# Retention one block at a time, strewn among the output projection and the last attention, with GpSimd's arithmetic moved elsewhere

## Chip, cores and metric

One core of a Trainium2 chip runs the whole layer. The metric is the device time of one execution in microseconds (us); the median of three runs of the kernel before is 2089.24 us. The engines are PE (matmul), DVE (vector), ACT (scalar), POOL (GpSimd) and SP, whose queue issues most of the plain transfers. Each engine takes its own instructions in the order in which they were written down for it.

## What is computed

One encoder layer over 2048 tokens of width 1024. Cut to what matters here:

```python
xn = rmsnorm(h, attn_norm_g)
q_da, k_da, v_da, q_r, k_r, v_r, g_r = split(xn @ w_in)
o_da = diff_attention(q_da, k_da, v_da, lam, da_subln_g)   # 4 heads, two score maps each, block-causal
o_r = retention(q_r, k_r, v_r, g_r)                        # 4 heads, below
h = h + concat(o_da, o_r) @ w_out
h = h + hier_moe(rmsnorm(h, ffn_norm_g))    # group top-1, expert top-2 of 32 SwiGLU experts
return rmsnorm(h, final_norm_g)

def diff_attention(...):            # per head
    a = p[:, :, 0] - lam * p[:, :, 1]                      # p: the two softmaxed maps
    return rmsnorm(a @ v, subln_g) * 0.8
def retention(q, k, v, g):          # per head, in chunks, decay gamma
    intra = ((q @ k.T) * 0.125 * where(rel >= 0, gamma**rel, 0)) @ v
    cross = (q * gamma**(pos + 1)) @ state
    state = state * chunk_decay + (k * 0.125 * gamma**(last - pos)).T @ v
    return silu(g) * head_rmsnorm(intra + cross)
```

All matrix products of the projections, the values and the experts are made of three matmuls, on a high and a low part of each operand (`mm3`, L62 to L64; `split_psum`, L54 and L55, makes the two parts of something that stands in PSUM).

## The kernel before

The program runs in stages, and a scheduler puts the instructions of each engine in order from a model of the time, with priorities given by the code.

Up to 735 us the input projection (`Proj`, L149 to L260) runs beside most of the attention. It writes q, k, v of the attention and, for retention, RT (q and k transposed), VR and GR to memory. `merge` (L564) mixes two streams of work by weights: the share FA = 0.7 of the attention goes beside the projection, FR = 0.12 beside retention, the rest beside the output projection. Attention runs in three stages over heads; per row block it makes scores (L350, L351, into pS), softmax (L352 to L366 on DVE and ACT), transposes (L382, into pT), values (into pO), and `finish` (L422 to L429) normalises by a Newton iteration and multiplies twice on POOL, by r (L426) and by the gain subg (L427).

Retention (L453) follows from 735 to 864 us. `prepare` loads two blocks of 128 tokens; POOL multiplies v (vd, L481) and q (qd, L486) by their decays; ACT and DVE make the gate th (L490, L491). Per block and pair of heads `inner` multiplies k by q (L499) and transposes k (L500) into one PSUM bank, DVE applies the decay matrix (A, L502) and ACT copies kd (L504); then come the outputs (L523, L524) and the state's increment (L528) in a second bank, which DVE adds to the state (L530). Three banks (pF) serve this. POOL normalises and gates two blocks (L549, L550).

Only then the eight tiles of w_out are loaded (L709) and split (L712 on ACT, L713 on POOL and DVE by turns). From 910 us on, the output projection (`OutProj`) goes block by block beside the last attention stage: `mx` loads a block, `mix` transposes and splits it, `half` multiplies by woh and wol into pF, DVE adds the residual (L747), then norm and router. It waits for attention rows through `k.ready` (L768). From block 12 on it has more PSUM banks (`widen`). The last attention matmul stands at 1168 us, the last block's residual at 1246.

The routing's end goes from 1246 to 1278: the last block's norm (ACT L835, POOL L836), counts and positions on DVE (L977 to L1064), then `route_finish`, which turns the lists by serial rounds of transpose (L1206), copy (L1208), matmul (L1210) and copy (L1211). The gather of the first expert's rows (L1518, POOL's indirect transfer) needs one of these. Weights of the first experts have been loaded ahead; their low parts `ml` are made early by POOL (L1484, L1487) and DVE (L1490).

From 1278 on 32 experts (`Moe`): rows gathered and turned (L1543, L1564), weights split (`mh` L1492 on ACT, `ml` L1493 on DVE), gate and up products, `hidden` (L1598: transposes L1604, then hhi and hlo by `split_psum`), down products, scattering (L1672). A normed and stored column of output runs beside: `f.square` (L1848), scale, store (L1864). In the end `down_last` (L1613) does the last expert and the last two columns, C14 and C15.

## Time and profile before

| | us |
|---|---|
| median of three runs (2086.17 to 2096.96) | 2089.24 |
| the profiled execution | 2073.39 |
| its span, first to last instruction | 2071.5 |
| PE busy | 1940.6 (94%) |
| DVE busy | 1554.3 (75%) |
| ACT busy | 1122.5 (54%) |
| POOL busy | 709.6 (34%) |
| mean granted TensorE clock | 0.975 |

The profiled execution was 15.85 us shorter than the median of the runs. Busy shares are means over the span; a stretch has to be read by itself. Matmuls are pipelined, and their durations overlap: what one costs where nothing waits is the distance between two starts. A releaser in brackets is what ended an engine's idle time.

### The profile page before, as it was taken

How to read it: one execution, taken by the hardware profiler on the slowest of the kernel's cores; microseconds unless marked ns; L12 is line 12 of the kernel's file. 1: busy time of each engine (PE TensorE's matmuls, PEld its weight loads, DVE VectorE, ACT ScalarE, POOL GpSimd, SP SyncE). 2: the span in 40 equal slices, each digit the busy share in tenths (PEclk: the TensorE clock that was granted, in tenths of full speed). 3: DMA queues.
4: the chain of work that ended last, by engine and by line, in shares of the span. 5: the costliest groups of instructions: out<-in, count | busy, mean ns of one | idle time of the engine just before them, and what ended most of it. 6: DMA issues, size and time to landing. Idle time of an engine off the chain costs nothing. (4 is left out here: it accounts for less than half of the span.)

```text
span 2071.5 us, 30117 instructions
## 1 busy us (share of the span) xinstructions
PE 1940.6 (94%) x9811; PEld 1542.1 (74%) x9811; DVE 1554.3 (75%) x3459; ACT 1122.5 (54%) x1915; POOL 709.6 (34%) x369
## 2 busy tenths in 40 slices
PE   7999999999999987789999996999999999999994
PEld 5788888788888875568887774777777677777673
DVE  7345446855566578987877777999998899898985
ACT  4244445544444454555454313776777777776773
POOL 0000000010000037421101106988756578686323
PEclk9999999999999999989999997999999999999997
DMA  6655344573675446464454453999999999999994
GB/s 202 198 150 171 117 133 141 184 236 127 205 214 168 139 154 217 129 198 143 138 171 132 144 227 129 321 321 341 313 322 328 328 321 349 343 356 302 329 309 125
DMA packets 241810, 459.61 MB, mean 222 GB/s; under 512 B 27376, under 2 KB 130160, under 8 KB 240624
## 3 DMA queue, kind: packets, MB, share of 16 engines
q1 hardware_dynamic: 224384, 401.53, 57.4%
q0 software_dynamic: 16976, 55.06, 9.9%
q8 instruction: 78, 1.28, 0.2%
q10 hardware_dynamic: 288, 1.05, 0.1%
q14 instruction: 84, 0.69, 0.1%
HBM read 365.81 MB, written 91.75 MB: 221 GB/s over the span
## 5 line engine op out<-in xcount | busy, mean ns | idle before, releaser
L1493 DVE TENSOR_TENSOR ml<-mr,mh 128x1024 fp32r<-128x1024 f32 x376 | 446.1, 1211 | 34.4 <-ACT mh L1492 34.2
L1492 ACT ACTIVATE mh<-mr 128x1024 fp32r<-128x1024 f32 x376 | 383.9, 1054 | 115.7 <-PE acc L74 70.5
L1525 POOL DMA_INDIRECT xg<-XN,TA x120 | 281.4, 2345 | 55.6 <-issue 30.8
L352 DVE CUSTOM_DVE_ANT_0 p<-pS,dist 128x512 f32<-128x512 f32 (+1 forms) x320 | 188.0, 605 | 124.8 <-PE pS L351 118.3
L426 POOL TENSOR_TENSOR U<-U,r 128x512 f32<-128x512 f32 (+2 forms) x13 | 16.5, 1271 | 724.8 <-DVE r L40 622.8
L359 ACT ACTIVATE p<-p,nm 128x128 f32<-128x128 f32 (+15 forms) x128 | 153.8, 1202 | 112.6 <-DVE nm L358 112.4
L62 PE MATMUL acc<-mh,xhi 128*128 128x512 f32 x512 | 204.7, 402 | 0.6 <-ACT xhi L1566 0.6
L63 PE MATMUL acc<-ml,xhi 128*128 128x512 f32 x512 | 204.1, 399 | 0.2 <-DVE ml L1493 0.2
L64 PE MATMUL acc<-mh,xlo 128*128 128x512 f32 x512 | 202.7, 397 | 0.7 <-DVE xlo L1567 0.7
L54 ACT ACTIVATE ah<-pT 128x512 fp32r<-128x512 f32 (+2 forms) x176 | 85.4, 498 | 139.2 <-PE pT L382 99.8
L62 PE MATMUL pa<-whi,xh 128*128 128x512 f32 x384 | 152.2, 398 | 3.0 <-ACT whi L161 2.3
L62 PE MATMUL pa<-xh,whi 128*128 128x512 f32 x384 | 152.7, 398 | 2.0 <-DVE st L58 2.0
L63 PE MATMUL pa<-wlo,xh 128*128 128x512 f32 x384 | 153.2, 400 | 1.5 <-DVE wlo L162 1.5
L64 PE MATMUL pa<-whi,xl 128*128 128x512 f32 x384 | 153.8, 401 | 0.0
L63 PE MATMUL pa<-xl,whi 128*128 128x512 f32 x384 | 152.0, 396 | 0.0
L64 PE MATMUL pa<-xh,wlo 128*128 128x512 f32 x384 | 151.7, 395 | 0.0
L350 PE MATMUL pS<-kst,qs 128*128 128x512 f32 (+1 forms) x320 | 124.7, 402 | 18.8 <-DVE cm L352 7.8
L162 DVE TENSOR_TENSOR wlo<-wr,whi 128x1024 fp32r<-128x1024 f32 x72 | 90.7, 1261 | 66.2 <-ACT whi L161 66.0
L55 DVE TENSOR_TENSOR al<-pT,ah 128x512 fp32r<-128x512 f32 (+2 forms) x176 | 97.5, 564 | 44.1 <-ACT ah L54 43.7
L62 PEld LDWEIGHTS acc<-mh,xhi 128*128 128x128 f32 x512 | 96.3, 188 | 31.8 <-ACT xhi L1566 0.7
L161 ACT ACTIVATE whi<-wr 128x1024 fp32r<-128x1024 f32 x72 | 76.1, 1058 | 80.1 <-DMA wr<-in_w_in_dram 39.9
L351 PE MATMUL pS<-kst,qs 128*128 128x512 f32 (+1 forms) x320 | 115.4, 376 | 0.0
(540 smaller groups left out, 4915.1 us busy)
## 6 DMA issues: line engine op xcount, KB each, us to landing
mr<-in_expert_w_gate_dram SPq DMA_DIRECT2D x128, 512.0 KB, 5.8
mr<-in_expert_w_up_dram SPq DMA_DIRECT2D x128, 512.0 KB, 6.2
mr<-in_expert_w_down_dram SPq DMA_DIRECT2D x128, 512.0 KB, 7.4
wr<-in_w_in_dram SPq DMA_DIRECT2D x72, 512.0 KB, 4.7
vst<-VS SPq DMA_DIRECT2D x72, 256.0 KB, 5.1
qs<-QS SPq DMA_DIRECT2D x128, 128.0 KB, 4.0
st<-in_x_dram SPq DMA_DIRECT2D x16, 512.0 KB, 4.2
VS<-st SPq DMA_DIRECT2D x32, 256.0 KB, 3.0
```

Of the source, the lines that this page charges most:

```text
L55: return nc.vector.tensor_sub(lo, ps, hi.bitcast(F32))
L62: nc.tensor.matmul(out, s_hi, m_hi, start=start, stop=False)
L63: nc.tensor.matmul(out, s_hi, m_lo, start=False, stop=False)
L64: nc.tensor.matmul(out, s_lo, m_hi, start=False, stop=stop)
L162: nc.vector.tensor_sub(lo, r, hi.bitcast(F32))
L350: nc.tensor.matmul(x, qs[0][:, m, 0, o:o + 128], ks[m][:, a0:a1], start=True, stop=False)
L351: nc.tensor.matmul(x, qs[0][:, m, 1, o:o + 128], ks[m][:, a0:a1], start=False, stop=True)
L352: nc.vector.tensor_tensor_reduce(p[:, a0:a1], x, tab[:, c0 + a0:c0 + a1], SLOPES[h], -3.0e38, OP.add, OP.max, accum_out=cm[:, n:n + 1])
L359: nc.scalar.activation(p[:, :nk], p[:, :nk], AF.Exp, bias=nm, accum_out=s0 if m == 0 else s1)
L1492: self.hi_at = nc.scalar.activation(hi, r, AF.Copy)
L1493: self.lo_at = nc.vector.tensor_sub(lo, r, hi.bitcast(F32))
L1525: nc.gpsimd.indirect_dma_start(out=xg[:, g * 256:(g + 1) * 256], out_offset=None, in_=v, in_offset=bass.IndirectOffsetOnAxis(ap=ix[:, g], ...
```

## The change

Retention is written for one block at a time, in `beside` with the last 0.3 of the attention, and both run beside the output projection. Keys are divided by their decay when the projection stores them (`key_decay`), so that q and v need no decay, the score needs only a mask, and the state's increment only a factor for each head (on ACT, while it copies kd). The norm's epsilon is scaled per row instead (`edec`). The gate is made when GR is stored, and applied by DVE, head by head. Retention has one PSUM bank (pR), the output projection two instead of three until `widen`; the last attention stage has smaller pools. w_out is loaded as soon as the projection ends; the gain subg goes into its first four tiles.

```diff
@@ Proj, storing RT and GR
+                nc.vector.tensor_mul(st..., ps..., k.kdec[:, ct - 2, None, :].to_broadcast([128, 4, 128]))
...
+                nc.scalar.activation(st, ps, AF.Tanh, scale=0.5)
+                nc.vector.scalar_tensor_tensor(st, st, 1.0, ps, op0=OP.add, op1=OP.mult)
@@ finish
-        nc.gpsimd.tensor_mul(u, u, r[:, :, None].to_broadcast([128, n, 128]))
-        nc.gpsimd.tensor_mul(u, u, k.subg[:, None, :].to_broadcast([128, n, 128]))
+        nc.vector.tensor_mul(u, u, r[:, :, None].to_broadcast([128, n, 128]))
-    step = 2 if (s, h) == (len(STAGES) - 1, 3) else nq
+    step = 2 if end else nq
@@ retention
-        G.tensor_mul(X.vd, ...)
...
-            G.tensor_mul(qd, ...)
...
+        pa = k.pR.tile([128, 512], F32, name="pR")
+        V.tensor_mul(A, pa[:, :256]..., k.msk[:, None, :].to_broadcast([128, 2, 128]))
+            nc.scalar.activation(kd[:, s], pa[:, 256 + 64 * s:320 + 64 * s], AF.Copy, scale=math.exp(128 * LGAM[2 * pr + s]))
...
-            G.tensor_mul(O, O, r[:, :, :, None].to_broadcast([128, 2, 4, 128]))
-            G.tensor_mul(O, O, X.th.rearrange("p a (h e) -> p a h e", h=4))
+        for h in range(4):
+            V.scalar_tensor_tensor(th[:, h], O[:, h], r[:, h:h + 1], th[:, h], op0=OP.mult, op1=OP.mult)
+        k.kept = b + 1
@@ OutProj
-BP = ((3, 2), (3, 1), (3, 2))
+BP = ((3, 2), (3, 1), (2, 1))
-        k.pF = pool("pF2", 3, space=PSUM)
+        k.pF = banks("pF2", 2)
+        k.pR = banks("pR", 1)
-        (nc.gpsimd if t % 2 < WOP else nc.vector).tensor_sub(lo, r, hi.bitcast(F32))
+            nc.scalar.activation(hi, r, AF.Copy, scale=k.subg)
+            nc.vector.scalar_tensor_tensor(lo, r, k.subg, hi.bitcast(F32), op0=OP.mult, op1=OP.subtract)
-            while b >= k.ready or b == LAST - 1 and not k.att_done:
+            while b >= min(k.ready, k.kept) or b == LAST - 1 and not (k.att_done and k.kept == NB):
-            nc.gpsimd.tensor_mul(xn, xn, k.ffg)
+            nc.vector.tensor_mul(hg, ht, k.ffg)
+            nc.scalar.activation(self.xn, hg, AF.Copy, scale=r)
@@ the stages
-        merge(tc, retention(k), 58, a, na * FR)
-        merge(tc, op.blocks(at), OB, a, na * (1 - FA - FR))
+        b = beside(retention(k), nr, a, ns)
+        merge(tc, op.blocks(at), OB, b, nr + ns)
```

In the routing's end, `route_finish` puts four transposes into one bank, copies them once and makes ten matmuls from the copy. All early weight splits are DVE's: three behind that copy, the rest behind the first rows' split.

```diff
@@ Moe
-            if 2 * q + part < EG:
-                nc.gpsimd.tensor_sub(lo, r, hi.bitcast(F32))
...
+            with k.tc.issue_after((k.turned if 2 * q + part < EL else k.split0).ins):
+                nc.vector.tensor_sub(lo, r, hi.bitcast(F32))
-        self.hl_at = split_psum(nc, X.hh, X.hl, pt)
+        self.hh_at = nc.scalar.activation(X.hh, pt, AF.Copy)
+        self.hl_at = nc.vector.tensor_sub(X.hl, pt, X.hh.bitcast(F32))
@@ the experts
+        with tc.high_priority(FIRST):
+            m.gather(jobs[0])
+            m.rows(jobs[0])
...
+                    with tc.high_priority(HID):
+                        m.hidden(jobs[n - 1])
...
-        with tc.issue_after(m.silu.ins):
+        m.hidden(X)
+        with tc.issue_after(m.hh_at.ins):
             f.square(C[13])
-        m.hidden(X)
+FIRST = 400
+HID = 200
```

The scheduler decides what this does to the order. First PE, before: a piece of the retention stretch. pS are attention scores, pT its transposes; the rest is retention.

```order
L382 MATMUL pT<-ident,p_7157 128x128 x2
L350 MATMUL pS<-kst,qs 128x512
L351 MATMUL pS<-kst,qs 128x512
L499 MATMUL pF<-qz_8149,kt 128x256
L500 MATMUL pF<-ident,kt 128x128
L523 MATMUL pF<-state_8155,qd_9150 128x128
L524 MATMUL pF<-vr,A 128x128
```

PE after, in the output projection beside the last attention. pF with woh and wol is the output projection, its L875 row the transposes for the router, pO the attention's values; L359 and L360 are its scores under their new line numbers.

```order
L62 MATMUL pF<-woh,mh 128x512
L63 MATMUL pO<-al,vst 128x128
L64 MATMUL pO<-ah,vst 128x128
L63 MATMUL pF<-wol,mh 128x512
L64 MATMUL pF<-woh,ml 128x512
L875 MATMUL pF<-ident,ht 128x128 x4
L527 MATMUL pR<-state_8190,qz_8194 128x128
L528 MATMUL pR<-vr,A 128x128
L530 MATMUL pR<-vr,kd 64x128
L359 MATMUL pS<-kst,qs 128x512
L360 MATMUL pS<-kst,qs 128x512
```

Retention's matmuls (pR) now stand in small groups between rows of the output projection and of attention. Next PE in the routing's end, ahead of the first expert, before: pF are the lists of `route_finish`, L1543 turns the first expert's rows.

```order
L1217 MATMUL pF<-P,LG 128x32 [waits Activation_49]
L1217 MATMUL pF<-P,LG 128x32 x3
L1206 MATMUL pF<-ident,aia 32x128
L1210 MATMUL pF<-P,atia_13367 128x32 [waits DVE_49]
L1206 MATMUL pF<-ident,aib 32x64 [waits PE_49]
L1210 MATMUL pF<-P,atib_13375 64x32 [waits DVE_49]
L1217 MATMUL pF<-P,LG 128x32 [waits Activation_49]
L1217 MATMUL pF<-P,LG 128x32
L1206 MATMUL pF<-ident,aib 32x64
L1210 MATMUL pF<-P,atib_13388 64x32 [waits DVE_49]
L1543 MATMUL pt<-ident,xg 128x128 [waits DMASW0_49,DVE_49]
```

And after, with L1226, L1238 and L1241 for the lists and L1561 for the rows:

```order
L1226 MATMUL pF<-ident,aia 32x128 [waits DVE_49,PE_49]
L1226 MATMUL pF<-ident,aia 32x128 [waits DVE_49]
L1226 MATMUL pF<-ident,aib 32x64 [waits DVE_49] x2
L1238 MATMUL pF<-P,at 128x32 [waits DVE_49]
L1238 MATMUL pF<-P,at 128x32
L1238 MATMUL pF<-P,at 64x32 x2
L1241 MATMUL pF<-P,LG 128x32 [waits Activation_49]
L1241 MATMUL pF<-P,LG 128x32 x3
L1241 MATMUL pF<-P,a_13574 128x32 [waits Activation_49]
L1241 MATMUL pF<-P,a_13574 128x32
L1561 MATMUL pt<-ident,xg 128x128 [waits DMASW0_49]
```

The serial rounds, each with a wait for DVE, have become one group; the turning of the rows waits for the gather alone. Last, ACT near the end, before: sg is the last expert's gate, fo the square of column C13, hhi the last hidden rows.

```order
L1658 ACTIVATE y<-acc 128x512 [waits PE_49]
L1585 ACTIVATE sg<-acc 128x512 [waits PE_49]
L1848 ACTIVATE fo,fs<-fh 128x1024 [waits DMASW6_49]
L54 ACTIVATE hhi<-pt 128x512 [waits DVE_49,PE_49]
L1630 ACTIVATE fo,fs_20994<-fh 128x512 [waits DMASW0_49,DVE_49,Activation_49]
L1630 ACTIVATE fo,fs_20994<-fh 128x512 [waits DVE_49]
L1633 ACTIVATE fo,fs_20995<-fh 128x1024 [waits DMASW1_49,Activation_49]
```

After:

```order
L1512 ACTIVATE mh<-mr 128x1024 [waits DMAHW2_49,DVE_49]
L1603 ACTIVATE sg<-acc 128x512 [waits PE_49]
L1623 ACTIVATE hhi<-pt 128x512 [waits PE_49]
L1872 ACTIVATE fo,fs<-fh 128x1024 [waits DMASW6_49]
L1650 ACTIVATE fo,fs_21198<-fh 128x512 [waits DMASW0_49,DVE_49,Activation_49]
L1652 ACTIVATE fo,fs_21199<-fh 128x1024 [waits DMASW1_49,Activation_49]
L1650 ACTIVATE fo,fs_21198<-fh 128x512 [waits DVE_49,Activation_49]
```

hhi (L1623) has moved ahead of the square of C13 (L1872).

## Rows read from the trace of the kernel before

**Rows 1.** Page: engine, busy us, share of the span, instructions.

```profile
PE 1940.6 (94%) x9811; PEld 1542.1 (74%) x9811; DVE 1554.3 (75%) x3459; ACT 1122.5 (54%) x1915; POOL 709.6 (34%) x369
```

**Rows 2.** Windows: length, busy PE, PEld, DVE, ACT, POOL, clock, DMA, GB/s.

```profile
735.00:864.00 129.00, 105.27 (x688) 83.93 (x687) 107.15 (x299) 69.10 (x252) 71.82 (x42) 0.95 0.55 175
864.00:910.00 46.00, 27.46 (x132) 22.37 (x130) 41.84 (x85) 23.76 (x48) 20.30 (x8) 0.74 0.54 183
...
735.00:905.00 170.00, 127.98 (x798) 102.57 (x797) 143.99 (x374) 88.75 (x289) 88.77 (x50) 0.90 0.56 179
...
910.00:1168.00 258.00, 251.14 (x1601) 211.93 (x1602) 194.46 (x559) 123.01 (x225) 37.44 (x30) 1.00 0.46 147
...
1246.00:1278.00 32.00, 13.64 (x65) 10.16 (x65) 24.10 (x101) 12.22 (x17) 17.62 (x9) 0.56 0.28 99
...
1290.00:1450.00 160.00, 154.82 (x688) 117.38 (x687) 159.50 (x214) 116.31 (x137) 142.01 (x53) 1.00 0.96 329
```

**Rows 3.** Timeline of PE, output projection: start us, us, engine, line, operation, tiles.

```profile
960.06 0.40 PE L62 MATMUL pF<-woh,mh 128*128 128x512 f32 x1
960.30 0.39 PE L63 MATMUL pF<-wol,mh 128*128 128x512 f32 x1
```

**Rows 4.** Timeline of PE, retention; a row with x2 holds two matmuls.

```profile
754.09 0.39 PE L523 MATMUL pF<-state,qd 128*128 128x128 f32 x2
754.31 0.39 PE L524 MATMUL pF<-vr,A 128*128 128x128 f32 x2
```

**Rows 5.** Waits, 735 to 910: who for whom, us in total, times, longest.

```profile
ACT junk L533 <- DVE state L530: 25.4, 14, 6.8
```

**Rows 6.** Timeline of SP's queue: start, time to issue, transfers.

```profile
879.25 20.62 SPq L709 DMA_DIRECT2D wor<-in_w_out_dram  x8
```

**Rows 7.** Groups on DVE by form, 735 to 905: busy us, mean ns, idle before.

```profile
L491 DVE SCALAR_TENSOR_TENSOR th<-th,gr 128x1024 f32<-128x1024 f32 x8 | 11.3, 1407 | 2.2 <-ACT th L490 2.2
L530 DVE SCALAR_TENSOR_TENSOR state<-state,sdec,pF 128x128 f32<-128x128 f32 x30 | 10.2, 339 | 6.0 <-PE pF L528 5.7
```

**Rows 8.** Line L363, 735:905, then 910:1168: ns minimum/median/maximum, first and last start.

```profile
L363 DVE SCALAR_TENSOR_TENSOR c<-c,S,nlam x6: 212/1124/1944, 751.6 to 891.1; 128x1 f32<-128x1 f32 x6
...
L363 DVE SCALAR_TENSOR_TENSOR c<-c,S,nlam x11: 204/221/1336, 914.6 to 1137.2; 128x1 f32<-128x1 f32 x11
```

**Rows 9.** POOL's costliest group, 735 to 905.

```profile
L550 POOL TENSOR_TENSOR O<-O,th 128x1024 f32<-128x1024 f32 x8 | 22.3, 2790 | 0.3
```

**Rows 10.** Timeline of DVE, routing end.

```profile
1250.95 2.23 DVE L990 TENSOR_TENSOR pen<-m,c 128x8 f32<-128x8 f32 x1
...
1260.38 2.33 DVE L1232 TENSOR_SCALAR aia<-RUN,ppia 128x32 f32<-128x32 f32 x1
...
1262.83 0.22 DVE L1232 TENSOR_SCALAR aib<-RUN,ppib 64x32 f32<-64x32 f32 x1
```

**Rows 11.** Timeline of POOL, routing end.

```profile
1250.81 2.34 POOL L836 TENSOR_TENSOR xn<-xn,ffg 128x1024 f32<-128x1024 f32 x1 [68.62 <-ACT xn L835]
1255.64 7.02 POOL L1484 TENSOR_TENSOR ml<-mr,mh 128x1024 fp32r<-128x1024 f32 x3 [2.49 <-ACT mh L1482]
1269.54 1.11 POOL L1518 DMA_INDIRECT xg<-XN,fia  x1 [6.88 <-PE pF L1206]
```

**Rows 12.** Timeline of PE, routing end; transfers, 1265 to 1280, us to landing.

```profile
1276.32 1.97 PE L1543 MATMUL pt<-ident,xg 128*128 128x128 f32 x8 [0.28 <-DVE wb L1211]
...
xg<-XN,fia POOLq DMA_INDIRECT x1, 4.5
```

**Rows 13.** Waits of PE, 1310 to 2037.

```profile
PE acc L64 <- DVE hlo L55: 6.9, 6, 2.6
```

**Rows 14.** Timeline, end of the program.

```profile
2041.48 1.06 ACT L1848 ACTIVATE fo<-fh 128x1024 bf16<-128x1024 f32 x1 [6.37 <-DMA fh<-H,perm]
...
2043.16 0.79 PE L62 MATMUL acc<-mh,hhi 128*128 128x512 f32 x1 [5.71 <-ACT hhi L54]
...
2044.19 1.00 POOL L1839 DMA_INDIRECT fh<-H,perm  x1 [5.24 <-DMA H<-y,ia]
```

More of the change, by code (lines that the diff above doesn't have):

```diff
@@ L445, in att_head @@
                 done += step
-                if step == 2:
+                if end and h == 3:
                     k.ready = 4 * g0 + done
@@ new lines, in load, with inner @@
+        return X
+    def inner(X, pr):
+        kT = X.kt[:, pr]
+        pa = k.pR.tile([128, 512], F32, name="pR")
+        nc.tensor.matmul(pa[:, :256], kT, X.q[:, pr], start=True, stop=True)
+        nc.tensor.transpose(pa[:, 256:384], kT, k.ident)
+        A = k.br.tile([128, 2, 128], F32, name="A")
+        V.tensor_mul(A, pa[:, :256].rearrange("p (s c) -> p s c", s=2), k.msk[:, None, :].to_broadcast([128, 2, 128]))
+        kd = k.br.tile([128, 2, 64], F32, name="kd")
+        for s in range(2):
+            nc.scalar.activation(kd[:, s], pa[:, 256 + 64 * s:320 + 64 * s], AF.Copy, scale=math.exp(128 * LGAM[2 * pr + s]))
+        return A, kd
@@ L517, in retention @@
+    nxt = load(0)
+    yield R0
+    for b in range(NB):
+        X = nxt
+        th = k.br.tile([128, 4, 128], F32, name="th", bufs=1)
+        nc.sync.dma_start(th, k.GR[X.ts, :].rearrange("p (h e) -> p h e", h=4))
+        O = k.br.tile([128, 4, 128], F32, name="O", bufs=1)
+        ss = k.br.tile([128, 4], F32, name="ss4")
+        st = []
+        for pr in range(2):
+            st.append(inner(X, pr))
+            yield 0.6
+        if b + 1 < NB:
+            nxt = load(b + 1)
         for pr in range(2):
@@ L902, in mixers @@
     with ExitStack() as ctx:
-        k.br = ctx.enter_context(tc.tile_pool(name="br", bufs=2, side="right", reuse_waits="tile"))
-        k.pF = ctx.enter_context(tc.tile_pool(name="pF", bufs=3, side="right", reuse_waits="tile", space=PSUM))
-        ret_consts(k)
-        merge(tc, retention(k), 58, a, na * FR)
-    with ExitStack() as ctx:
+        k.kept = 0
         op = OutProj(k, ctx, outer)
@@ new lines, in route_finish @@
+    p4 = ps()
+    o = 0
+    for i, (tab, p0, n, idx, w) in enumerate(lists):
+        for c in range(2):
+            x = 64 * i + 32 * c
+            nc.tensor.matmul(p4[:n, x:x + 32], at[:, o:o + n], k.P, start=True, stop=True)
+            o += n
+    for g in range(6):
+        nc.tensor.matmul(p4[:, 128 + 32 * g:160 + 32 * g], a4[g // 4][:, g % 4 * 128:g % 4 * 128 + 128], k.P, start=True, stop=True)
+    for i, (tab, p0, n, idx, w) in enumerate(lists):
+        q = (k.TA if idx == "ia" else k.TBw).bitcast(I32)[:, 0:n // 32]
+        setattr(k, idx + "q", q)
+        V.tensor_scalar(q, p4[:, 128 + 128 * i:128 + 128 * i + n].rearrange("p (g e) -> p g e", e=32), 4.0, k.quad,
+                        op0=OP.mult, op1=OP.add)
```

325 lines of the change are left out of this document (144 added, 181 removed).

## The prediction, made before the changed kernel had run

> **What bounds the kernel now.** I read the busy shares first: PE is busy 94% of the span and DVE 75% [rows 1], so a gain must come out of a stretch in which PE stands still or works thinly. The windows by stage name two such stretches [rows 2]. From 735 to 905 us (retention with some attention, then the wait for w_out) PE is busy 128 of 170 us at a mean granted clock of 0.90, with POOL busy 88.8 us; from 1246 to 1278 (the end of the routing) PE is busy 13.6 of 32 us, at 0.56. From 910 to 1168 (output projection with the last attention) it is busy 251 of 258 at 1.00.
>
> Busy time flatters PE, since ends are modelled. I therefore count its dense content: so many matmuls from the instruction order, times their spacing where nothing waits. That spacing is 0.23 us for 512 columns [rows 3] and 0.11 us for a retention matmul of 128 columns (pairs 0.22 apart) [rows 4]. 735 to 864 then holds 92 us of PE work in 129, 864 to 910 holds 15 in 46, 910 to 1168 about 243 in 258: 350 us of work in 433, or 81%. What PE lacks up to 864 is shown by who waits: ACT stood 25.4 us for DVE's state update, 14 times, the longest 6.8 [rows 5]. From 864 to 910 PE lacks w_out: SP spends 20.6 us issuing its eight loads, from 879.25 on [rows 6].
>
> **Retention in the output projection.** PE's retention work stays: 64 matmuls of 256 columns at 0.22, 280 of 128 at 0.11, 60 for the state at about 0.16, in all 54 us. It was packed between 735 and 864; by the new order it is strewn between attention scores and w_out matmuls. Counted in the new order, PE has 19.5 us of dense work between the projection and the first w_out matmul, 301 from there to the last retention matmul and 32 to the last attention matmul: 352, as before. Each piece is priced by its own limit.
> - Head: 19.5 us of PE, but about 39 of DVE (eight splits of w_out and the attention beside them), and 20.6 of SP for w_out before that. I take 45 us; the bounds are 39 (DVE alone) and 60 (w_out's 20.6 first, DVE's 39 behind it).
> - Mixed part: 301 us at an efficiency that no row shows. Neighbours are 71% (735 to 864) and 94% (910 to 1168). I take 91%, near the second, because the queued w_out matmuls are there to fill, as they were after 910, but one retention bank and two instead of three for w_out are less freedom: 331 us.
> - Tail: 32 of PE against 46 of DVE: 48.
>
> The sum is 424 against 433, -9. Behind the last attention the order has 61 us of PE work up to the experts where it had 67: -6. Region: **-15**, from -42 (head 39, 97%) to +27 (head 60, 84%).
>
> This needs DVE to have room, for all that GpSimd did now falls on it, ACT or nobody. Before, DVE was busy 107+42+194 = 343 us from 735 to 1168 [rows 2]. Added: 64 gating operations at 0.34 (the nearest row is the 128x128 state update) are 22, four more w_out splits at 1.4 (the 128x1024 row) are 6, more normalisations of the last attention 8. Moved into the projection: eight operations of 1.41 us [rows 7], -11; there they become 24 shorter ones, in a stretch where DVE has room and PE doesn't wait for it, so I cost them at 0 (bounds -3 and +3; without that cover, 14). Given back: DVE is slower next to POOL. A one-column operation (L363) takes 0.22 us at the median in the output projection and 1.12 in retention, with a longest of 1.94 [rows 8]; POOL's own run up to 2.8 us [rows 9]. The excess of every DVE form over the same form elsewhere, added up in this way, is 33 us, of which these six make 5. DVE ends at about 335 us in 424: 79%, as busy as before (343 in 433), so I keep it off the path except in head and tail.
>
> The Trainium skill (SBUF — State Buffer, "SBUF: two separate sides") says that DVE and GpSimd share a port pair as an exclusive lock, so that the loser stands for the whole instruction. The L363 row agrees in kind. By that rule alone up to the whole POOL time of the stretch, 88.8 us, could come back to DVE instead of 33, and nothing of DVE's would be late; the sum keeps 33.
>
> Retention's loads go from two blocks to one (SP has some 70 issues more). SP is not what ends PE's waits there, so 0, bounds -1 and +4: behind w_out's loads in SP's queue now stand the first block's loads, inside the head's 45.
>
> **Routing tail.** DVE's small operations stretch beside POOL: 2.23 us for an 8-column one, and three others up to the 32-column 2.33, whose twin takes 0.22 [rows 10]. Beside them POOL runs the last normed block and three weight splits [rows 11]. The four cost 8.9 us and alone 0.7: -8.2, on the chain to the gather's index. The gather is issued at 1269.54, but PE turned the rows only at 1276.32, because four serial rounds of transpose, copy and matmul stood before it (released by the last copy, not by the gather) [rows 12]. Batched, those rounds end first, and the gather's landing (4.5 us after issue) decides: 1269.5-8.2+4.5 = 1265.8, 10.5 earlier. Then 1.5 goes back: three more splits at 1.4 us fall on DVE behind the first split of rows, where DVE is busy 159.5 of 160 us [rows 2], and PE only partly hides it. **-9**, from -12 to -4.
>
> **Experts and end.** The transposes of the hidden rows come earlier; PE waited 6.9 us in six places for the lower half of the split [rows 13]: **-5**, bounds -9 and +4 (earlier transposes can push a weight split behind on a full DVE). At the end ACT stood for a load until 2041.48 with the hidden rows' split queued behind it, and PE until 2043.16, 5.7 us idle [rows 14]. The new order puts that split first. But the next block's load is issued at 2044.19, when the scatter of the rows before has landed, and the last adds wait for it as they do for PE: I count 2 of the 5.7. **-2**, from -4 to 0. The remaining small moves lie on no chain that the trace shows: 0.
>
> **The sum.** -15-9-5-2 = -31 us, 2073.39 to about 2042 for the profiled execution. That one lies 15.85 us (0.8%) below the median of the runs, 2089.24; I take the same difference off the median: **2058 us**. Something like 0.5%, 10 us, is what a measurement here can tell from no change.
>
> **Rivals.**
> *A, the mixed part runs dense.* If the freed DVE and the strewn retention let PE run at 97% with a head of 39 us, the region is 39+310+46 = 395, less 6: -44 and in all -60, 2029. If both happen in part, -45. For: 910 to 1168 had 94% with DVE at 75%, and of POOL's 88.8 us more than 33 may come back to DVE. Against: one retention bank, two w_out banks. 0.20.
>
> *B, retention is only moved.* Head and tail, both at DVE's pace, take back what the stretch of 735 to 905 gives: region 0 (head 58, 90% in between, tail as forecast, -6 behind), half of the routing's gain lost on a DVE that is full from 1290 on, the earlier transposes nothing, the end -2: -6, 2083. For: DVE has 39 and 46 us in head and tail, and K, V and w_out loads fall together. Against: the routing's rows are plain. 0.18.
>
> *C, slower: the one retention bank.* PE takes its instructions in order. A block passes the bank four times, 64 times in all, and PE stands until DVE and ACT have emptied it. In the new order most passes are 1.5 to 10 us of other PE work apart, about a dozen less than 1. Emptying takes at least the 0.34 of DVE and ACT's copies behind it; a DVE that is 80% full adds what is queued ahead, and one long row operation is over 2 us. At 0.5 us a pass the forecast holds (its 30 us of loss). From about 1 us a pass (61 lost, the forecast's 30 and its gain of 31) the kernel is slower than before; at 1.3, 83 are lost and it ends at 2111. For: the retention stretch itself worked so, at 71%, with three banks. Against: the spacing. 0.09.
>
> There PE would also stop shortly and often. In 735 to 905 its mean granted clock was 0.90, against 1.00 afterwards [rows 2]. The Trainium skill (TensorE: Matmul & The Clock Gate, "A second HAM failure mode: psum-queue depth-cycling") tells of a kernel in which cycling through PSUM banks left PE such short idles that the clock kept falling; by that rule, an estimate, a mixed part at 0.90 would cost up to a tenth of its 301 us more. The trace shows the lower clock beside longer waits too, so I leave it inside C.
>
> **How the numbers follow.** Forecast 0.53 (2045 to 2074: the region from -28 to 0, the rest as summed), A 0.20, B 0.18, C 0.09. Faster by over 0.5% takes the forecast and A but for a small part of the forecast's upper edge, and a little of B: 0.75. Same: 0.16. Slower: C, 0.09. For 8 in 10 the range reaches through A's middle and B: 2020 to 2090, leaving out the far end of A and C.
>
> **What would show it.** First w_out matmul near 780; last attention matmul near 1160; PE busy shares above 9 tenths between them at a clock of 1.00, with waits for pR of a few us in all. L363 back at 0.22 everywhere. DVE from the last residual add to the expert's first transposes without a 2 us row, the transposes some 10 us closer, released by the gather. No wait of 5 us ahead of the last down matmuls. Waits on pR or A of tens of us would show C; a head over 55 us shows B. The prediction is wrong if the projection up to 735 or the weight-bound experts move by more than 5 us, for which I see no reason.

## The result and the profile after

The changed kernel took 2139.96 us (median of four runs, 2126.19 to 2147.03) against 2088.77 us before: a ratio of 1.0247, interval 1.0209 to 1.0284. It is slower by 51 us, and the forecast was 31 us faster. The profiled execution took 2136.21 us, its span 2134.4, where before had 2071.5. The spans differ by 63 us and not by 51 because the profiled execution of before lay some 15 us below its median, that of after 4 us below.

To see where the 63 us between the two spans lie, I cut both traces at the same events of PE (its first or last matmul of a kind):

| stretch | before, us | after, us | difference |
|---|---|---|---|
| start to last projection matmul | 734.7 | 762.8 | +28.1 |
| to first w_out matmul (head) | 175.8 | 48.8 | |
| to last retention matmul (mixed) | | 353.4 | |
| to last attention matmul (tail) | 255.0 | 62.0 | |
| from the projection's end to the last attention matmul | 430.8 | 464.3 | +33.5 |
| to last w_out matmul | 79.6 | 83.3 | +3.7 |
| to first expert matmul | 33.0 | 26.1 | -6.9 |
| to last expert matmul | 772.9 | 771.1 | -1.8 |
| to the end | 20.5 | 26.8 | +6.3 |

One trace stands behind each column. How firm the rows are is shown by traces with the same order on PE: two versions of before that are edited only from the routing on (below) end the projection at 736.4 and 735.7 and take 431.2 and 435.1 us to the last attention matmul, so the left column holds within 5 us there. The changed kernel and five edits of it that leave PE's order in the projection as it is end it between 754.0 and 763.5, so its +28.1 may be 19 to 29.

The windows of after, by stage, with the columns of [rows 2]:

```profile
0.00:763.00 763.00, 728.62 (x3621) 608.96 (x3622) 452.02 (x1260) 333.85 (x666) 7.10 (x48) 0.98 0.54 164
763.00:812.00 49.00, 35.01 (x159) 25.81 (x157) 33.01 (x98) 21.68 (x58) 0.00 (x0) 0.69 0.84 259
812.00:1165.00 353.00, 330.26 (x2021) 269.59 (x2020) 254.50 (x888) 162.58 (x420) 26.02 (x20) 0.98 0.47 148
1165.00:1227.00 62.00, 45.43 (x267) 35.84 (x265) 41.91 (x119) 26.45 (x50) 4.59 (x4) 0.81 0.14 49
1227.00:1310.00 83.00, 72.58 (x364) 55.61 (x365) 55.82 (x302) 14.19 (x33) 0.00 (x0) 0.90 0.53 194
1310.00:1337.00 27.00, 14.11 (x70) 10.62 (x69) 19.80 (x107) 12.49 (x18) 8.38 (x5) 0.61 0.28 93
```

POOL is out of the way, as it was to be, and DVE has what was forecast (33+254.5+41.9 = 329 us, 335 forecast). The head is 49 us long (45 forecast). But the mixed stretch is 353 instead of 331, the tail 62 instead of 48 at a granted clock of 0.81, and the projection, for which nothing was forecast, is 28 us longer. DVE's stretching beside POOL, on which part of the gain was to rest, is indeed gone: the one-column operation of [rows 8] and the 8-column one of [rows 10] read, in after (minimum/median/maximum ns),

```profile
L372 DVE SCALAR_TENSOR_TENSOR c<-c,S,nlam x16: 211/216/221, 816.1 to 1198.8; 128x1 f32<-128x1 f32 x16
...
L1009 DVE TENSOR_TENSOR pen<-m,c x1: 156/156/156, 1316.3 to 1316.3; 128x8 f32<-128x8 f32 x1
```

So that mechanism works, and the kernel lost elsewhere. Splitting PE's time tells how. For each form of matmul I took its usual distance to the next start (the 30th percentile in that trace, or the distance itself where shorter) as its work, the time in which PE was empty as idle, and the remainder as rest (half clock, waits inside the pipeline):

| from the projection's end to the last attention matmul | length | work | idle | rest |
|---|---|---|---|---|
| before | 430.8 | 307.5 | 49.2 | 74.1 |
| after | 464.3 | 328.2 | 53.3 | 82.7 |

Two things are seen: idle and rest, 123 us before, are 136 now, not less; and nearly the same matmuls (2441 records where before had 2404) have become 21 us more work. The idle time has changed its kind: 31.5 us of it ended at an operation of DVE before and 18.0 after, 8.9 us at a load before and 22.0 after. The experiments take these one by one, then the projection and the routing. Stretches are quoted by their cuts: "projection" is the time of its last matmul, "mixed stretch" is from there to the last attention matmul (464.3 in the changed kernel).

### The profile page after: what moved, and what is told of

Same layout as the page of the kernel before. It is cut to its first block, busy times and chain, and to the rows that moved or that the text cites. A ratio compares the mean times of both kernels' runs of the same rounds, so it can differ in the third digit from the quotient of the medians.

```text
span 2134.4 us, 30383 instructions
## 1 busy us (share of the span) xinstructions
PE 1982.5 (93%) x9811; PEld 1564.9 (73%) x9811; DVE 1563.1 (73%) x3684; ACT 1118.5 (52%) x1927; POOL 575.9 (27%) x293
## 4 chain that ended last, share of the span: by engine, by line
PE 76%; DMA 9%; DVE 5%; issue 4%; POOL 2%; ACT 2%; SPq 1%; DVEq 0%; ACTq 0%; POOLq 0%
PE pa L62 7%; PE pa L63 7%; PE pa L64 7%; PE acc L63 7%; PE acc L64 7%; PE acc L62 7%; PE acc L72 4%; PE acc L74 3%; PE pS L359 3%; PE pF L62 3%; PE pF L63 3%; PE pF L64 3%; PE pS L360 3%; PE pT L391 2%; PE pO L63 1%
## 5 line engine op out<-in xcount | busy, mean ns | idle before, releaser
L1543 POOL DMA_INDIRECT xg<-XN,TA x120 | 272.2, 2268 | 54.0 <-issue 30.5
L359 PE MATMUL pS<-kst,qs 128*128 128x512 f32 (+1 forms) x320 | 124.4, 404 | 27.8 <-DMA qs<-QS 14.6
L887 POOL TENSOR_TENSOR xc<-xT 128x512 bf16<-128x512 f32 x24 | 30.6, 1277 | 432.4 <-ACT xT L884 429.4
```

What stands on the lines that cost most here:

```text
L359: nc.tensor.matmul(x, qs[0][:, m, 0, o:o + 128], ks[m][:, a0:a1], start=True, stop=False)
L1543: nc.gpsimd.indirect_dma_start(out=xg[:, g * 256:(g + 1) * 256], out_offset=None, in_=v, in_offset=bass.IndirectOffsetOnAxis(ap=ix[:, g], ...
```

## Experiments on the mixed stretch

**The state's matmuls.** In the new text each head's increment (L530, 64 rows of output) stands behind that head's output; before, both heads' increments stood together (L528). The edit puts them together again:

```diff
-                if b < NB - 1:
-                    nc.tensor.matmul(po[s * 64:(s + 1) * 64, 256:384], kd[:, s], v, start=True, stop=True)
             if b < NB - 1:
+                for s in range(2):
+                    h = 2 * pr + s
+                    nc.tensor.matmul(po[s * 64:(s + 1) * 64, 256:384], kd[:, s], X.vr[:, h * 128:(h + 1) * 128], start=True, stop=True)
```

> The two matmuls that make the state's increment of a pair of heads (64 output rows each, in two halves of the bank) stand next to each other again behind the outputs, as before the change, instead of one behind each head's output. Theory P (adjacent they run at the same time on two halves of the array; apart each takes its own 0.16 us and more): these 120 matmuls, 30.9 us from start to next start in the changed kernel, fall to 18 to 22, the stretch from the projection's end to the last attention matmul from 464 to 450 to 458, total -6 to -13. Rival: the waits around them take the time instead, and the stretch stays within 4 us.

The mixed stretch fell to 449.8 (-14.5), its work to 310.3; the total to 2121.9 us (ratio to before 1.0147, 1.0103 to 1.0191). Timelines of PE, first the changed kernel, one pair of heads, then this one:

```profile
871.64 0.38 PE L527 MATMUL pR<-state,qz 128*128 128x128 f32 x2
871.86 0.39 PE L528 MATMUL pR<-vr,A 128*128 128x128 f32 x2
872.18 0.43 PE L530 MATMUL pR<-vr,kd 128*64 128x128 f32 x2
872.54 0.49 PE L527 MATMUL pR<-state,qz 128*128 128x128 f32 x2
872.86 0.39 PE L528 MATMUL pR<-vr,A 128*128 128x128 f32 x2
873.18 0.43 PE L530 MATMUL pR<-vr,kd 128*64 128x128 f32 x2
```

```profile
864.48 0.38 PE L527 MATMUL pR<-state,qz 128*128 128x128 f32 x2
864.70 0.39 PE L528 MATMUL pR<-vr,A 128*128 128x128 f32 x2
864.92 0.39 PE L527 MATMUL pR<-state,qz 128*128 128x128 f32 x2
865.14 0.39 PE L528 MATMUL pR<-vr,A 128*128 128x128 f32 x2
865.46 0.44 PE L532 MATMUL pR<-vr,kd 128*64 128x128 f32 x4
```

A pair takes 1.9 us in the first (871.64 to the end of 0.36 us behind 873.18), 1.4 in the second. One such matmul shows as two records, so 120 records are 60 matmuls, and a row with x2, in [rows 4] too, is one matmul. The increments of both heads, four records, end in 0.44 us when adjacent, and their starts lie 0.01 us apart by twos; alone, the two records of one take 0.36 to the next start. Over all 120 records the distances to the next start sum to 17.6 us before, 30.9 after and 21.7 here. Theory P holds, and it is most of the 21 us of added work (17.9 go with this edit).

**The order of output projection and attention.** OB is the weight of the output projection in `merge`; a smaller one lets attention and retention go ahead.

```diff
-OB = 200
+OB = 150
```

> The weight OB of the output projection in the merge is 150 instead of 200, so attention and retention run earlier beside it. Theory T: the stretch from the last retention matmul to the last attention matmul (62 us) shrinks below 50 and the whole by 10 to 20 us. Theory S: the order of loads is as crowded, total within 6 us of the changed kernel. Theory B: within 6 us.

Total 2123.14 us (1.0185, 1.0122 to 1.0247), mixed stretch 445.2 (-19), idle in it 40.6 instead of 53.3; the part that ended at a load is 9.4 us instead of 22.0. The tail did not shrink (75 us, since retention ends earlier), so theory T is right about the knob and wrong about the place. What the wait rows of PE show (us in total, times, longest) is fewer waits for loads of qs and kst (those for mx stay: 5.6 us); after, then this run:

```profile
PE pS L359 <- DMA qs<-QS: 11.8, 5, 4.4
PE pT L391 <- DVE p L375: 7.6, 2, 6.0
PE pS L359 <- DMA kst<-KS: 5.2, 1, 5.2
PE pF L765 <- DMA mx<-MIX: 5.1, 3, 2.4
...
PE pR L528 <- ACT O L536: 3.1, 1, 3.1
```

```profile
PE pS L359 <- DMA qs<-QS: 4.2, 2, 4.0
PE pS L359 <- DMA kst<-KS: 3.9, 1, 3.9
```

**The one retention bank** (rival C of the prediction).

```diff
-            po = k.pR.tile([128, 512], F32, name="pR")
+            po = k.pR.tile([128, 512], F32, name="pF")
...
-        k.pF = banks("pF2", 2)
-        k.pR = banks("pR", 1)
+        k.pF = k.pR = banks("pF2", 3)
```

> Retention and output projection share three PSUM banks (pF) instead of one and two. Theory B (one retention bank makes PE wait): total 10 to 30 us less than the changed kernel, in the stretch from the projection's end to the last attention matmul. Theories S and T: within 6 us, since PE's waits for pR sum to some 10 us in the changed kernel.

2137.06 us (1.0279, 1.0218 to 1.034), mixed stretch 459.2. Within the 6 us that the other theories gave; rival C falls. PE's waits had said so: in the changed kernel those for pR sum to 9.7 of 53 us, and the longest is the 3.1 above.

**SP's queue.** Between 860 and 1140 us SP stood 57 us (20 times) for buffers of retention's q loads, with loads of attention queued behind. The loads kt, qz, vr and th go to POOL's queue:

```diff
-            nc.sync.dma_start(X.kt[:, pr], k.RT[2 + pr][:, ts])
+            nc.gpsimd.dma_start(X.kt[:, pr], k.RT[2 + pr][:, ts])
...
```

> Retention's loads (kt, qz, vr, th) are issued by POOL instead of SP; nothing else is edited. Theory S (SP's queue: retention's loads wait there for free buffers, and the loads of attention and output projection stand behind them; PE waits for those loads and runs at half clock after): from the end of the projection to the last attention matmul 464 us become 430 to 445, PE's waits for qs, kst and mx fall from some 20 us to under 8, total 20 to 30 us less than the changed kernel. Theory T (the last attention runs alone at the end, since the output projection has used up its blocks): 464 stays within 6 us. Theory B (one retention bank): stays within 6 us.

2141.24 us (1.0275, 1.0224 to 1.0326), mixed stretch 469.1. Theory S, my first after the result, falls. The same with the stores that wait for DVE (GR and both halves of MIX):

```diff
-            nc.sync.dma_start((k.VR if c == 4 else k.GR)[bs, :], st)
+            (nc.sync if c == 4 else nc.gpsimd).dma_start((k.VR if c == 4 else k.GR)[bs, :], st)
...
-        nc.sync.dma_start(k.MIX[X.ts, 512:1024], th.rearrange("p h e -> p (h e)"))
+        nc.gpsimd.dma_start(k.MIX[X.ts, 512:1024], th.rearrange("p h e -> p (h e)"))
```

> The changed kernel with the stores that wait for DVE (the gate GR in the projection, both halves of MIX) issued by POOL instead of SP. Theory Q (these stores hold SP's queue while they wait for DVE, weight and key loads stand behind them, and PE waits): the projection ends at 745 to 752 instead of 754 to 763, the stretch to the last attention matmul falls by 8 to 20 from 464, total 2115 to 2130. Rival: as with retention's loads, nothing changes by more than 6 us, since other waits take the place.

2138.43 us (1.0233, 1.0202 to 1.0264), projection 761.1, mixed stretch 464.0: the rival. Taking these waits out of SP's queue gives PE nothing.

**Together.** Pairs, lambda's tile (below), OB = 150, and the early splits behind the first rows (below):

> The changed kernel with four of the edits tried together: the state's matmuls in pairs, lambda's own tile in the first two stages, OB = 150, early splits behind the first rows. If the gains add up (-14 in the stretch by the pairs, -5 at the start by lambda, -19 by OB, -2 by the splits): total about 2095 to 2105, from the projection's end to the last attention matmul 425 to 435, level with the kernel before or up to 1% slower. If they are one gain seen several times (the last attention's order): total 2110 to 2120.

2110.99 us (1.012, 1.0088 to 1.0152): projection 751.3, mixed stretch 432.9, experts 790.0. The mixed stretch is now level with before (430.8); the expected 2095 to 2105 was missed by what the experts lost. A good part of that came with the fourth edit: PE's first 96 expert matmuls took 48.5 us instead of 38.1, with a hole of 12.65 us that is explained with the early splits below. The version without that edit was not run. On this one three more; first a smaller OB:

```diff
-OB = 150
+OB = 100
```

> The version with four edits with OB = 100 instead of 150. Theory T (attention ends late because the output projection has used up its blocks): the stretch from the projection's end to the last attention matmul falls from 433 to 410 to 425, total -8 to -20 against 2111. Rival: at OB = 150 this is spent; total within 6 us of 2111 or longer, because then output projection work is left for later with nothing beside it.

2115.93 us (1.0145, 1.0117 to 1.0173), mixed stretch 433.8: the knob is spent. Then the three shared banks:

```diff
-        k.pF = banks("pF2", 2)
-        k.pR = banks("pR", 1)
+        k.pF = k.pR = banks("pF2", 3)
```

> The version with four edits with three PSUM banks shared by retention and output projection. Theory B: -5 to -15 against 2111, in the stretch to the last attention matmul. Rival: within 5 us.

2113.83 us (1.0131, 1.0099 to 1.0162), mixed stretch 441.6: no gain here either. And the stores on POOL, as above:

> The version with four edits (pairs, lambda, OB = 150, early splits behind the first rows; 2111 us) with the same three kinds of stores on POOL. Theory Q: 2090 to 2103, of which the projection -5 to -10. Rival: within 6 us of 2111.

2119.7 us (1.016, 1.0128 to 1.0192), projection 759.5, mixed stretch 429.1. Theory Q falls again; with 8.7 us more than without the edit the total is not within the rival's 6 either.

Two things of the change in this stretch were taken back in no run: the smaller pools of the last attention stage (`BP`), and the state's decay as a factor on ACT.

## Experiments on the projection

**Lambda's tile.** In the changed kernel the four lambda vectors have no tile of their own; they lie in oT's buffer.

```diff
-    lam = k.bo.tile([128, 4, 64], F32, name="lam", tag="oT")
+    lam = k.bc.tile([128, 4, 64], F32, name="lam") if n < 2048 else k.bo.tile([128, 4, 64], F32, name="lam", tag="oT")
```

> In the first two attention stages lambda's vectors have a tile of their own again instead of oT's buffer. Theory L (the projection ends 20 to 28 us late since SP's queue stands at lambda's loads, with weight loads behind them): the projection ends at 745 or earlier (changed kernel: 754 to 763 in five looks). Rival: within 3 us of that band; then the stores of the gate, the smaller pool of attention's small tiles or the added DVE work are left.

2119.18 us (two runs; 1.015, 1.0105 to 1.0196). PE at the start, in the changed kernel and here:

```profile
25.34 0.80 PE L62 MATMUL pa<-whi,xh 128*128 128x512 f32 x1 [5.49 <-ACT whi L161]
```

```profile
21.47 0.49 PE L62 MATMUL pa<-whi,xh 128*128 128x512 f32 x1 [2.27 <-ACT xh L54]
```

The hole at 25 us is gone, and the 192nd projection matmul starts at 70.4 us instead of 74.7 (70.0 before). The projection as a whole ended at 755.2, so theory L covers 4 to 5 us and no more. That the mixed stretch came out at 447.0 (-17) follows from no mechanism of this edit, which touches only the two stages before it. The scheduler's order there is another one, and this is the size that its order alone can have: the work stays as it is, idle falls from 53 to 44 us and rest from 83 to 74. The -19 of OB = 150 is of the same kind, so that it comes from OB's weight, and not from just another order, is not shown. The pairs' gain is shown by the fall of the work (17.9), though the order around them changed too.

**The attention's small tiles** (four instead of three in the first two stages):

```diff
-    k.bsm = pool("bsm", 3)
+    k.bsm = pool("bsm", 4 if s < 2 else 3)
```

> The pool of attention's small tiles (bsm) has four buffers again in the first two stages. Theory M (softmax chains beside the projection wait for a free small tile, and PE for softmax): the projection ends at 745 or earlier, where the changed kernel has 754 to 763. Rival: within 3 us of that band.

2140.8 us (two runs; 1.0254, 1.0209 to 1.0299), projection 762.8. No effect.

**The gate**, from both sides. In the changed kernel, made in retention again (the projection stores GR by an ACT copy; retention loads it, tanh and product there):

```diff
-                nc.scalar.activation(st, ps, AF.Tanh, scale=0.5)
-                nc.vector.scalar_tensor_tensor(st, st, 1.0, ps, op0=OP.add, op1=OP.mult)
+                nc.scalar.activation(st, ps, AF.Copy)
...
-        nc.sync.dma_start(th, k.GR[X.ts, :].rearrange("p (h e) -> p h e", h=4))
+        gr = k.br.tile([128, 4, 128], F32, name="O", bufs=1).rearrange("p h e -> p (h e)")
+        nc.sync.dma_start(gr, k.GR[X.ts, :])
+        nc.scalar.activation(th.rearrange("p h e -> p (h e)"), gr, AF.Tanh, scale=0.5)
...
```

> The gate is made in retention again: the projection stores GR as it comes (ACT copy), retention loads it, ACT takes tanh and DVE the product per block. Theory G (the projection ends 28 us later because stores of the gate wait for DVE in SP's queue, and the weight loads behind them come late): the projection ends 10 to 20 us earlier than at 762.8, total -5 to -15. Rival L (the projection's loss comes from the lambda loads that share a buffer with oT, and from more attention beside it): the projection ends within 5 us of 762.8, total 0 to +8.

2141.37 us (1.0277, 1.0226 to 1.0329), projection 754.0, mixed stretch 474.6. The stretch from the 1152nd to the 1344th projection matmul shrank from 76.2 to 68.1 us (66.9 before), but runs without this edit ended at 754 to 755 too (retention's loads on POOL, three shared banks), so the end decides nothing. And in the kernel before, the gate alone moved into the projection:

```diff
-            nc.scalar.activation(st, ps, AF.Copy)
+            if c == 4:
+                nc.scalar.activation(st, ps, AF.Copy)
+            else:
+                nc.scalar.activation(st, ps, AF.Tanh, scale=0.5)
+                nc.vector.scalar_tensor_tensor(st, st, 1.0, ps, op0=OP.add, op1=OP.mult)
...
-        X.th = k.br.tile([128, 2, 512], F32, name="th")
-        nc.scalar.activation(X.th, gr, AF.Tanh, scale=0.5)
-        V.scalar_tensor_tensor(X.th, X.th, 1.0, gr, op0=OP.add, op1=OP.mult)
```

> The kernel before with one part alone: the gate is made when the projection stores GR, and retention loads it ready. Theory G: the projection ends 6 to 12 us later than at 734.7, most of it between 361 and 428 us, and retention gains a few us; total 0 to +10. Rival: the projection ends within 3 us of 734.7.

2125.27 us (1.0196, 1.0142 to 1.025): this one part, which takes an ACT and a DVE operation out of retention, costs 37 us. The projection ended 7 us later (741.7), as theory G had it, though it was only 1 us late at 428 us; but from its end to the first w_out matmul it took 210.5 us instead of 175.8, where a gain was expected. PE's groups in that stretch:

```profile
L354 PE MATMUL pS<-kst,qs 128*128 128x512 f32 x54 | 28.2, 533 | 20.5 <-DVE cm L356 13.5 <-DMA qs<-QS 4.7 <-DMA kst<-KS 2.4
...
L500 PE MATMUL pF<-qz,kt 128*128 128x256 f32 x64 | 23.3, 448 | 12.8 <-ACT O L536 11.4 <-DVE qz L468 0.9 <-DMA qz<-RT 0.5
```

434 attention matmuls lie in it where before had 346, and PE stood 13.5 us for the softmax (cm) and 11.4 for ACT's copies of O. The edit changed the order far from its own place. Part of the 35 us is attention that came earlier: at the last attention matmul 19 of them are left (450.1 instead of 430.8), which is still almost three times the 7 of the projection. The experts took 788.5 us instead of 772.9, with no edit of theirs.

**The work that moved to DVE.** On the version with four edits, U's multiplication goes back to POOL; then also the gate to retention:

```diff
-        nc.vector.tensor_mul(u, u, r[:, :, None].to_broadcast([128, n, 128]))
+        nc.gpsimd.tensor_mul(u, u, r[:, :, None].to_broadcast([128, n, 128]))
```

> The version with four edits (2111 us, projection's end at 751.3) with the multiplication of U by r in the attention's finish on POOL again. Theory V (DVE is full for some 12 us where a stage of the attention ends beside the projection, at 362 to 374, and PE waits for softmax and weights behind the 1.22 us of U and the gate's products): the projection ends at 742 to 748. Rival: within 3 us of 751; POOL's operation stretches DVE's small ones instead.

2124.11 us (1.0164, 1.0116 to 1.0212), projection 754.0 (751.3 without the edit), mixed stretch 446.2: no gain in the projection, and 13 us more behind it. This is g1_upool; the second edit on top of it:

> As g1_upool, and the gate is made in retention again, so that of the work moved to DVE beside the projection only the keys' decay is left there. Theory V: the projection ends at 738 to 745 (before 734.7, and some 5 us of attention more beside it now), and the mixed stretch takes 5 to 12 us more than 433, for it does the gate. Rival: the projection ends within 3 us of 751.

2137.06 us (1.0216, 1.0166 to 1.0265), projection 756.7, mixed stretch 450.5, 18 us more than 433. Theory V falls, though DVE is indeed full where an attention stage ends (12.72 of 14 us in the version with four edits):

```profile
361.00:375.00 14.00, 11.39 (x58) 9.13 (x57) 12.72 (x39) 8.27 (x19) 0.00 (x0) 0.88 0.71 218
```

## Experiments on routing, experts and end

**Routing alone**, in the kernel before (route_finish in one batch, all early splits on DVE, the last norm without POOL; hunks of the change's own diff), of which these lines matter below:

```diff
-EP = 6
...
-            if 2 * q + part < EG:
-                nc.gpsimd.tensor_sub(lo, r, hi.bitcast(F32))
```

> The kernel before with the routing's end alone as changed: one batch of transposes and matmuls in route_finish, the early weight splits and the last block's norm without POOL. Theory R (that part gains what the changed kernel shows there): from the last w_out matmul to the first expert matmul 33 us become 24 to 27, and total -4 to -8 against before. Rival: the splits that move to DVE cost the experts what is gained: total within 2 us of before.

2096.96 us (1.005, 1.0029 to 1.0071): the routing took 26.3 us instead of 33.0, as theory R had it, and the kernel is 0.5% slower all the same. From the first expert matmul to the 97th it took 43.0 us instead of 26.7 (38.1 in the changed kernel). PE, then DVE behind it, in this run:

```profile
1316.09 0.60 PE L1283 MATMUL pt<-u_tri,u_w 32*128 32x32 f32 x2 [12.85 <-DVE u_w L1292]
```

```profile
1291.27 2.34 DVE L1486 TENSOR_TENSOR ml<-mr,mh 128x1024 fp32r<-128x1024 f32 x2
1297.15 2.29 DVE L1555 STREAM_TRANSPOSE xT<-xg 128x1024 f32<-128x1024 f32 x1 [3.54 <-DMA xg<-XN,TA]
1299.36 0.10 DVE L1272 TENSOR_SCALAR u_u<-u_u 32x1 f32<-32x1 f32 x1
1299.39 3.48 DVE L1486 TENSOR_TENSOR ml<-mr,mh 128x1024 fp32r<-128x1024 f32 x3
...
1311.68 0.72 DVE L1577 SCALAR_TENSOR_TENSOR sg<-sg,wa,acc 128x512 f32<-128x512 f32 x1
1312.33 2.34 DVE L1486 TENSOR_TENSOR ml<-mr,mh 128x1024 fp32r<-128x1024 f32 x2
1314.60 1.21 DVE L1558 TENSOR_TENSOR xlo<-xT,xhi 128x1024 fp32r<-128x1024 f32 x1
1315.74 0.21 DVE L1280 COPY u_w<-u_u 32x128 f32<-32x128 f32 x1
```

A chain of small operations for the later lists (u_u to u_w) is strewn between the splits. A transposition waits 3.54 us in DVE's queue for gathered rows, everything behind it too; and PE, in order, stands 12.85 us at a 32-column matmul that needs u_w. Behind it stand the transposes of the first expert's gate sg. DVE makes sg only at 1311.68, among the same splits, so by these rows PE would have stood some 9 us without the small chain too, and u_w adds the last 4. In the changed kernel PE's holes there are 1.09 us (for the rows' low part), 4.17 (for a weight split) and 3.40 (for u_w).

**Splits beside the gather** (EL from 3 to 0, so none runs while the first gather is issued):

```diff
-EL = 3
+EL = 0
```

> All early weight splits on DVE come behind the first rows' split (EL = 0), none while the first gather runs. Theory W (the three splits beside the gather hold POOL up while it writes the gather's descriptors: 4.59 us of POOL time in the changed kernel, 1.11 before): the gather takes 1.0 to 1.3 us of POOL, the first rows are turned 3 to 3.5 us earlier after the last residual; the splits then come later, so that the time from the last residual to a full run of experts gains 0 to 3 us. Rival: POOL's span there is no work of its own and the turning stays where it is.

POOL's gather, in the changed kernel and here:

```profile
1326.81 4.59 POOL L1538 DMA_INDIRECT xg<-XN,fia  x1 [102.21 <-PE pF L1226]
```

```profile
1325.61 1.11 POOL L1538 DMA_INDIRECT xg<-XN,fia  x1 [102.29 <-PE pF L1226]
```

The three splits (3.47 us on DVE from 1326.92) had held POOL's gather: theory W holds for the gather, and the routing took 24.1 us instead of 26.1. The whole stayed where it was (2141.77 us, two runs; 1.0259, 1.0214 to 1.0303): with more splits behind the first rows, PE now stood 12.38 us at the matmul for u_w, where the changed kernel has 3.40, and came to its 97th expert matmul after 49.2 us instead of 38.1.

**The small reorderings alone**, in the kernel before:

> The kernel before with the small reorderings alone: priority of the first gather and of the hidden rows, and the order in the last job. Theory H (the prediction's): PE's waits for the lower half of the hidden rows go, total -3 to -9. Rival E (what the changed kernel shows: other waits for weight splits come instead, and the end waits for the scatter and the load behind it): total within 3 us of before, and from the last gate to the end 37 us as before.

2091.88 us, 1.0005 (0.9976 to 1.0034): nothing. Rival E has it. PE's waits for hlo [rows 13] are gone in this run, and these stand in their place (1310 to 2037 us, as there):

```profile
PE acc L63 <- DVE ml L1493: 4.7, 8, 1.5
PE acc L71 <- DVE hv L55: 4.7, 1, 4.7
```

In the changed kernel the end shows why nothing is won there. PE's wait of [rows 14] is gone (the last job's first down matmul has 0.69 us before it instead of 5.71), but the load of the last column still follows the scatter, as in the third row of [rows 14], and the adds wait for it:

```profile
2101.01 1.60 POOL L1688 DMA_INDIRECT H<-y,ia  x1 [0.30 <-issue]
2107.73 0.99 POOL L1863 DMA_INDIRECT fh<-H,perm  x1 [5.12 <-DMA H<-y,ia]
...
2112.99 0.69 DVE L1648 TENSOR_TENSOR fh<-fh,acc 128x512 f32<-128x512 f32 x1 [5.56 <-DMA fh<-H,perm]
```

From the last gate (sg) to the end it is 37.0 us before and 37.5 after.

## Why the prediction was wrong

- **"Mixed part: 301 us at 91%."** The step that failed first is the one ahead of it, "PE's retention work stays", 54 us. I had counted matmuls and multiplied; the increments' price was read from neighbours that stand in pairs, and the new order has no pairs. The term was 60 at 0.16, 9.6 us; between starts they take 17.6 us before and 30.9 after. That is 13 us more, and 14.5 us of the stretch when undone.
- **The efficiency itself.** I took it near that of 910 to 1168, "because the queued w_out matmuls are there to fill". Here they did not: PE takes them in the written order. The mixed part had 301 of 353, 85%; and with the pairs, OB and lambda's tile the whole stretch is at 432.9 (429.1 at best, with the stores on POOL) against 430.8: in the best order that I found, strewing retention gains nothing against doing it ahead of the output projection. That is rival B's outcome for this stretch, though not by its terms (its head was 58 us, measured 49). The idle time before w_out, 42 us that seemed free for the taking, came back as waits of 1 to 6 us for qs, kst, mx and softmax. For slower than before I gave 0.09, and all of it to rival C, which fell: the way in which it became slower was in none of my rivals.
- **The tail**, 48 forecast, 62 measured: DVE's 46 us were right (41.9), but what was left to do kept neither DVE nor PE (45.4 of 62) busy, at a granted clock of 0.81. What bounds it was not tested; its length moves with the order (41 to 95 us over the runs).
- **DVE**, on which I spent most of the working, was sized rightly (335 forecast, 329 measured) and did not decide: PE's idle time behind it fell by 13.5 us in the stretch, and that behind loads, which has no term in the sum, rose by 13.1.
- **Rival C** fell by two runs. The granted clock from 812 to 1165 was 0.98. So the lower clock that the Trainium skill tells of for cycling through PSUM banks (TensorE: Matmul & The Clock Gate, "A second HAM failure mode: psum-queue depth-cycling") isn't seen here.
- **SP at 0** stands for retention's loads and the stores: both were moved away without effect.
- **The projection at 0** is the largest miss of one term (+28 in this trace), and the prediction had named a move of more than 5 us there as a sign of being wrong. Lambda's loads are 4.5 of it, and some 5, by an estimate from their number and spacing, are attention matmuls that now run beside it (384 instead of 372 score records by its end). The gate alone, in the kernel before, is 7. The rest arises between 361 and 636 us, where PE was idle for 13 us instead of 6 and the granted clock was 0.97 instead of 1.00; no single edit took it away: neither stores, small tiles, U, nor the gate here. Its cause stays open. The keys' decay, retention's first loads and the output projection's setup, all now issued inside the projection, were not taken out one by one.
- **Routing -9**: the stretched rows went as forecast (from the last w_out matmul to the gather's issue 16.4 us instead of 24.4, forecast 8.2 less), and the stretch gave -6.9; splits beside the gather kept 2 of the rest. "Then 1.5 goes back" was too small by a factor of nearly 8: the first 96 expert matmuls take 11.4 us more (16.3 with the routing alone). I had priced the DVE work that moves, 3 splits, and not what now queues behind and between them on DVE and holds PE up: weight splits, the first expert's gate and the small chain.
- **Hidden rows -5, end -2**: 0 when tried alone. The hidden rows' wait was real, and other waits, for weight splits and for another low part, took its place.

Over all: 28.1 + 33.5 + 3.7 - 6.9 - 1.8 + 6.3 make the span's 63, where the forecast had 0, -15 for the next two together, -9, and -7 for the last two together. In the -1.8 of the experts lie the first 96 matmuls' +11.4 and -13.2 behind them. No run explains the shorter remainder, and it is in part luck of this execution: 733 us, where three edits of the changed kernel with the same order on PE there have 737 to 742 (before: 746). The whole stretch took 771 to 798 us over all kernels here.

## What to carry to other kernels

Idle time of PE beside a stage is not a hole that other work falls into: the gain of interleaving is read from what PE waits for there and whether the filler has other waits, and filler with a chain of its own brings these along. Work that moves to another engine costs also what then stands behind it in that engine's order. Count matmuls in the order in which they will stand, since some are cheap only next to their twin. Where a scheduler writes the order, an edit of one operation can cost several times its price far from its place; measure each part alone before adding them up, as the gate (1.0196) and the routing (1.005) by themselves would have told.

## What the runs showed of the hardware that I had not expected

Two matmuls with 64 output rows each, on partitions 0 to 63 and 64 to 127 of one bank, ran together when adjacent (four records in 0.44 us, starts 0.01 us apart by twos) and one after the other when another stood between (0.36 us for the two records of each). An indirect gather took 4.59 us on POOL while DVE ran three subtractions with both inputs in SBUF, and 1.11 without them. The Trainium skill (SBUF — State Buffer, "SBUF: two separate sides") describes such a lock for a DVE operation with two inputs in SBUF against a POOL operation that reads SBUF, and the row agrees in kind; that it is the gather's own reading that waits, no run here shows. Runs of one kernel spread by about 1% here, 2126 to 2147 us for the changed kernel, with the projection's end at 754 or 763 in kernels whose text there is the same.
